# Half-width diagonal score blocks for the linear attention, and idle matmuls in the first half unit of a two-layer trunk

## The chip, the cores and the metric

One core of a Trainium2 chip runs the whole program; the other seven are idle. The metric is the device time of one execution in microseconds (us). TensorE is called PE here, VectorE DVE, ScalarE ACT, GpSimd POOL and SyncE SP, as in the profile; PEld is PE's weight loads.

## What is computed

The reference runs two layers on 256 tokens of width 1024. Each layer projects the normalised input, runs four attention branches of four heads, gates and sums them, and ends with an MLP of squared ReLUs. The change touches the linear-attention branch (GLA), whose scores within a chunk carry a decay for each key channel:

```python
def gla_chunked(q, k, v, log_a):
    ...
    b = jnp.cumsum(_chunk(log_a, c), axis=-2)
    causal = jnp.tril(jnp.ones((c, c), dtype=bool))
    decay = jnp.exp(jnp.where(causal[:, :, None], b[..., :, None, :] - b[..., None, :, :], -jnp.inf))
    scores = jnp.einsum('nbhic,nbhjc,nbhijc->nbhij', qc, kc, decay)
    o_intra = jnp.einsum('nbhij,nbhjd->nbhid', scores, vc)
    ...

def hybrid_layer(...):
    ...
    for n, o in enumerate((o_sb, o_gla, o_dn, o_dil)):
        merged = merged + gates[:, :, n] * (o.reshape(B, S, BRANCH_WIDTH) @ w_branch[n])
    x = x + merged @ w_out
    h = rms_norm(x, g_mlp)
    return x + jnp.square(jax.nn.relu(h @ w_mlp_in)) @ w_mlp_out
```

## The kernel before

Every weight matrix is read once, as a row of "units" (`UNITS`), each of two halves of 512 KB. A half arrives by DMA in a tile `raw` (six buffers). It is then split in two numbers that PE multiplies quickly: ACT casts the upper part `whi` (L254), DVE subtracts it from `raw` for the remainder `wlo` (L255). The activations are split likewise (`ah`, `al`; for a branch's output `oh`, `ol`). PE then makes three products for each half: `whi` by `ah`, `whi` by `al`, `wlo` by `ah`, accumulated in a PSUM bank with the tag `bg`. A gate or projection half is 24 matmuls of 256 columns. `half` asks for splits three halves ahead (`LEAD`).

The attention branches are Python generators (`dn_chain`, `sb_chain`, `dil_chain`, `gla_chain` and helpers) in four threads. `small()` runs after each half unit and advances every thread by one step; `yield from pause(name)` adds as many empty steps as the table `PAUSE` says. The scheduler is off (`manual_schedule`), so this sets the order of each engine's instructions by hand. The order of units in a layer is `SEQ`: projections, then for each branch four gate units and the branch's own unit (`unit_br`), in the order SB, DIL, DN, GLA. `unit_br` first calls `finish(n)`, which forces what is left of that branch's chain, and then multiplies the branch's output by its weights, four pairs of columns (`fp` 0 to 3), each evacuated by DVE (`gt`, L1311).

`gla_chain` builds the transposed scores of a layer in `ST`, a tile of 128 partitions by 3 blocks by 4 heads by 128 columns; blocks 0 and 2 are the diagonal blocks of tokens 0 to 127 and 128 to 255, block 1 the one off the diagonal. POOL clears blocks 0 and 2 (L1070 and the line after it). Coarse blocks are copied from PSUM by ACT. The diagonal and its next neighbours come by two masked copies of DVE (L1110, 128 partitions by 1024 elements each). The levels of 2 to 16 tokens come as small matmuls in the two PSUM banks with the tag `fb`, two heads at a time (`hp` 0 and 1), one bank for each head `b`. For each bank DVE then makes eight masked copies (L1126): four levels, each for the partitions 0 to 63 and 64 to 127, because the two halves write other columns of `ST`. After pause `g9` the second bank follows one step later. The matmuls of `hp` 1 need both `fb` banks again. At the end PE multiplies `v` by `ST` (the only matmuls `fb<-s,sb_k`), and `head_rms` normalises the result: a square on ACT (L584), a sum over heads on PE (`fb<-dlT,C`), `v` on DVE (L593), two activations on ACT (L316, L317), three steps and a product on DVE (L326 to L328, L598), and the split in `oh` (ACT, L474) and `ol` (DVE, L475), which the GLA unit's matmuls read.

At the start of the program, in `trunk`, ten matmuls on a tile of zeros run while the first data are on their way (`WARM`). The first unit (`unit_F` with `boot`) then follows the input and weights as they land, piece by piece, 16 matmuls `whi`/`wlo` by `ah` for its first half (`ft` 0), then 8 by `al`. The masks arrive as f32 in two DMAs of 384 columns and POOL casts them to bytes (L1190).

Of the kernel before, what the change touches and what calls it, by code (L numbers as in the profile page):

```python
# [11 lines left out]
BF = mybir.dt.bfloat16  # L12
U8 = mybir.dt.uint8
# [25 lines left out]
EVU = [3, 3]  # L39
KNOBS = {'SQE': (0, 1), 'CD': (2, 3, 4, 5), 'BSQ': ((2, 2, 2, 2), (2, 0, 2, 0), (0, 0, 0, 0), (2, 2, 0, 0), (0, 2, 0, 0), (2, 0, 0, 0), (1, 2, 2, 0), (1, 2, 0, 0), (2, 2, 0, 1)), 'NPOOL': (0, 1), 'MROWS': (1, 2), 'MADD': ((1, 1, 1, 1), (1, 0, 1, 1), (0, 1, 0, 1), (0, 0, 1, 1), (1, 0, 0, 1)), 'MLO': ((1, 1, 1, 1), (1, 0, 1, 1), (0, 1, 1, 1), (0, 1, 0, 1), (1, 0, 0, 1)), 'DENP': (0, 1), 'TWO': (0, 1), 'ROWS': 'pair', 'TMP': 'pair', 'FLIP': 'pair', 'EVU': 'pair'}  # L40
PAIRS = {'ROWS': (2, 3), 'TMP': (3, 4, 5, 6), 'FLIP': ('dn_v', 'sb_q', 'sb_k'), 'EVU': (0, 1, 2, 3)}
PAUSE = {'m0': 0, 'm1': 0, 'dS': 1, 'd1': 1, 'd2': 2, 'd3': 1, 'd13': 0, 'd14': 0, 'd15': 1, 'd16': 0, 'd17': 2, 'd21': 0, 'd22': 1, 'd23': 1, 'd24': 1, 'd25': 1, 'd26': 0, 'd27': 0, 'd28': 1, 'd29': 0, 'd30': 1, 'd31': 0, 'd32': 1, 'd33': 0, 's0': 2, 's1': 1, 's2': 0, 's3': 1, 's4': 0, 's5': 1, 's6': 0, 's7': 1, 's8': 0, 's9': 1, 's10': 1, 'l0': 2, 'l1': 1, 'l2': 0, 'l3': 1, 'l4': 1, 'l5': 0, 'l6': 2, 'l7': 0, 'l8': 0, 'l9': 2, 'l10': 0, 'l11': 0, 'l12': 1, 'l13': 3, 'g0': 1, 'g1': 0, 'g2': 0, 'g3': 4, 'g4': 1, 'g5': 0, 'g6': 1, 'g7': 1, 'g8': 2, 'g9': 1, 'g10': 0, 'g11': 0, 'fa0': 0, 'fa1': 0, 'fa2': 0, 'fa3': 0, 'fa4': 1, 'fb0': 0, 'fb1': 1, 'fb2': 0, 'fb3': 1, 'fb4': 3, 'd20': 0, 'd34': 0, 'u31': 0, 'u30': 0, 'u29': 0, 'u28': 1, 'u27': 2, 'u26': 0, 'u25': 1, 'u24': 0, 'u23': 0, 'u22': 1, 'u21': 0, 'u20': 2, 'u19': 0, 'u18': 4, 'u17': 2, 'u16': 0, 'u15': 1, 'u14': 0, 'u13': 0, 'u12': 0, 'u11': 1, 'u10': 2, 'u9': 2, 'u8': 0, 'u7': 0, 'u6': 1, 'u5': 0, 'u4': 0, 'u3': 2, 'u2': 0, 'u1': 1, 'dr': 0, 'dl': 1, 'hfa': 1, 'hfb': 0, 'l15': 1, 'e4': 1, 'e5': 0, 'e6': 0, 'e7': 1, 'e8': 0, 'e9': 1, 'e10': 0, 'e12': 0, 'eE0': 2, 'eE1': 0, 'eE2': 1, 'd4': 0, 'e3': 0, 'g12': 1, 'q0': 0, 'q1': 1, 'q2': 1, 'q3': 5, 'q4': 4, 'q5': 0, 'l16': 0, 'l17': 1, 'g13': 0, 'g14': 3, 'g15': 0, 'v_mini': 0, 'v_sb_k': 0, 'v_sb_v': 0, 'v_dil_q': 0, 'v_dil_k': 0, 'v_dil_v': 0, 'v_gla_q': 0, 'v_gla_v': 0, 'v_gla_r': 0, 'v_dn_gate': 0, 'v_dn_v': 0, 'x_hy': 0, 'x_hz': 0, 'x_ht': 0, 'x_x0': 0, 'x_x1': 0, 'x_pt': 0, 'x_s0': 0, 'x_s1': 0, 'x_s2': 0, 'x_ut': 0, 'x_mc': 0}

OFF = {"sb_q": 0, "sb_k": 256, "sb_v": 512, "gla_q": 768, "gla_k": 896, "gla_v": 1024, "gla_lr": 1280,
       "gla_r": 1296, "dn_q": 1552, "dn_k": 1808, "dn_v": 2064, "dn_a": 2320, "dn_b": 2324, "dn_gate": 2328,
# [41 lines left out]
def constants():  # L87
    j = np.arange(128)[:, None]
    i = np.arange(128)[None, :]
    c = np.zeros((128, NCON), np.float32)  # L90
    c[:, C_ID:C_ID + 128] = i == j
    c[:, C_NEGU:C_NEGU + 128] = -1.0 * (j >= i)
    c[:, C_NEG1:C_NEG1 + 128] = -1.0
    c[:, C_UT:C_UT + 128] = j <= i
    c[:, C_GT:C_GT + 128] = j > i
    c[:, C_STR:C_STR + 128] = j < i
    c[:, C_SBN:C_SBN + 128] = np.where(j < i, 0.0, NEG)
    for b, d in enumerate((j - i, j + 128 - i, j - i)):
# [84 lines left out]
def trunk(ctx: ExitStack, tc: tile.TileContext, xin, w, par, con, msk, out, dbg=None, nl=NL):  # L183
# [20 lines left out]
    def mm(o, l, r, start=True, stop=True):  # L204
        PE.matmul(o, l, r, start=start, stop=stop, skip_group_check=True)  # L205
# [354 lines left out]
    def mixing(l, pr, mp, nm):  # L560
# [503 lines left out]
        def gla_chain():  # L1064
# [1 line left out]
            F, qk = got["F"], got["gla_qk"]  # L1066
            yield from pause("g12")
            ST = T([3, 4, 128], "s6")
            POOL.memset(ST[:, 0], 0.0)
            POOL.memset(ST[:, 2], 0.0)  # L1070
            yield from pause("g5")
            for hp in range(2):

                pss = [bank("fb") for _ in range(2)]
                rows = [slice(32 * hh, 32 * hh + 32) for hh in (2 * hp, 2 * hp + 1)]
                for r, ps in zip(rows, pss):
                    mm(ps[:, 0:128], F[r, 0, 0:128], F[r, 0, 128:256])
                for t in range(2):
                    c = 128 * t
                    for r, ps in zip(rows, pss):  # L1080
                        mm(ps[0:64, 128 + 64 * t:192 + 64 * t], F[r, 1, c:c + 64], F[r, 1, c + 64:c + 128])
                for t in range(2):
                    c = 128 * t
                    for b in (0, 64):
                        for r, ps in zip(rows, pss):
                            mm(ps[b:b + 32, 256 + 32 * t:288 + 32 * t], F[r, 2, c + b:c + b + 32],
                               F[r, 2, c + b + 32:c + b + 64])
                yield from pause("g6")
                for hh, ps in zip((2 * hp, 2 * hp + 1), pss):
# [289 lines left out]
```

## Time and profile before

| what | us |
|---|---|
| three runs: median (lowest to highest) | 899.93 (899.72 to 901.83) |
| the profiled execution's own time | 898.36 |
| its span, first to last instruction | 896.5 |
| PE busy in the span | 867.0 (97%) |
| DVE, ACT, POOL busy | 640.8, 537.4, 137.8 |
| mean granted clock of TensorE | 0.98 of 2.4 GHz |

The three parts of the profile used below are the timeline (one line for each run of like instructions: start, length, engine, line, operation, out<-in, number; the bracket is the engine's idle time before it and who ended it), the windows (busy time of each engine in a stretch, and PEclk, the granted clock: 1.00 is 2.4 GHz, 0.50 is 1.2 GHz) and the waits (who waited for whom). Line 205 is the helper of all matmuls, so they are told apart by their operands. An f32 matmul shows as several records.

### The profile page before, as it was taken

The numbers are of one execution on the slowest core, as the hardware profiler recorded it, in microseconds if no ns is written. First come the engines' busy times: TensorE is split into PE (matmuls) and PEld (weight loads), VectorE is DVE, ScalarE is ACT, GpSimd is POOL, SyncE is SP. The second block draws the span as 40 slices with busy tenths as digits, with TensorE's granted clock in tenths as the row PEclk, the third lists the DMA queues.
The fourth block names the chain that finished last, engine by engine and source line by source line (L and its number), as shares of the span: only waits on it lengthen the run. The fifth ranks groups of instructions, "written<-read, shape, count | busy, mean of one in ns | idle before, by whom it ended". The sixth has DMA issues, their size and how long they took to land.

```text
span 896.5 us, 19105 instructions
## 1 busy us (share of the span) xinstructions
PE 867.0 (97%) x7758; PEld 840.4 (94%) x7758; DVE 640.8 (71%) x1272; ACT 537.4 (60%) x846; POOL 137.8 (15%) x142
## 2 busy tenths in 40 slices
PE   7899999998999999999989999999989999999998
PEld 5898999998999999999989899999989999999998
DVE  5878999448788677644488799983596877665442
ACT  4687767855655665633368777696655555664331
POOL 3513401122012000000052341013030120000000
PEclk7899999998999999999999999999999999999999
DMA  8554354543445566665444445554344636667641
GB/s 267 203 157 151 119 189 142 165 142 114 146 145 207 174 202 193 216 219 193 154 158 131 158 135 164 166 159 133 114 140 160 219 122 194 204 204 231 197 148 48
DMA packets 43432, 149.80 MB, mean 167 GB/s; under 512 B 4944, under 2 KB 7248, under 8 KB 43344
## 3 DMA queue, kind: packets, MB, share of 16 engines
q1 hardware_dynamic: 43056, 148.42, 51.1%
q8 instruction: 61, 1.00, 0.5%
q14 instruction: 27, 0.22, 0.1%
q10 hardware_dynamic: 288, 0.17, 0.1%
HBM read 147.52 MB, written 1.05 MB: 166 GB/s over the span
## 4 chain that ended last, share of the span: by engine, by line
PE 72%; DVE 17%; ACT 4%; issue 3%; POOL 2%; DMA 2%; SPq 0%; DVEq 0%; ACTq 0%
PE bg L205 45%; PE fa L205 14%; PE fb L205 12%; DVE wlo L255 5%; DVE al L352 2%; DMA raw<-w 2%; POOL s L382 1%; DVE s L1126 1%; DVE d L706 1%; ACT whi L254 1%; DVE x L516 1%; DVE ush L781 1%; DVE ush L779 1%; DVE Y L783 1%; DVE al L389 1%
## 5 line engine op out<-in xcount | busy, mean ns | idle before, releaser
L255 DVE TENSOR_TENSOR wlo<-raw,whi 128x1024 fp32r<-128x1024 f32 (+2 forms) x280 | 340.9, 1239 | 157.3 <-ACT whi L254 156.8
L254 ACT CAST whi<-raw 128x1024 fp32r<-128x1024 f32 (+2 forms) x280 | 283.4, 1037 | 119.4 <-PE bg L205 60.9
L205 PE MATMUL bg<-ah,whi 128*128 128x256 f32 (+1 forms) x1296 | 316.9, 285 | 3.0 <-ACT whi L254 1.9
L205 PE MATMUL bg<-al,whi 128*128 128x256 f32 (+1 forms) x1296 | 296.6, 279 | 1.8 <-DVE al L352 1.8
L205 PEld LDWEIGHTS bg<-ah,whi 128*128 128x128 f32 (+1 forms) x1296 | 246.0, 190 | 10.5 <-ACT whi L254 3.2
L205 PEld LDWEIGHTS bg<-al,whi 128*128 128x128 f32 (+1 forms) x1296 | 237.9, 189 | 3.2 <-DVE al L352 2.4
L205 PE MATMUL bg<-ah,wlo 128*128 128x256 f32 x1280 | 189.7, 280 | 1.5 <-DVE wlo L255 1.5
L205 PEld LDWEIGHTS bg<-ah,wlo 128*128 128x128 f32 x1280 | 168.5, 191 | 2.6 <-DVE wlo L255 2.5
L205 PE MATMUL fa<-uh,whi 128*128 128x256 f32 x256 | 70.4, 276 | 0.0
L205 PE MATMUL fa<-uh,wlo 128*128 128x256 f32 x256 | 70.4, 276 | 0.0
L205 PE MATMUL fa<-ul,whi 128*128 128x256 f32 x256 | 69.7, 276 | 0.0
L205 PE MATMUL fb<-uh,whi 128*128 128x256 f32 x224 | 61.6, 276 | 0.0
L205 PE MATMUL fb<-uh,wlo 128*128 128x256 f32 x224 | 61.6, 276 | 0.0
L205 PE MATMUL fb<-ul,whi 128*128 128x256 f32 x224 | 61.0, 276 | 0.0
L543 ACT ACTIVATE sq<-rl 128x512 f32<-128x512 f32 x32 | 20.3, 633 | 66.4 <-DVE rl L542 66.4
L1312 POOL TENSOR_TENSOR mg<-mg,gt 128x512 f32<-128x512 f32 x20 | 31.5, 1594 | 150.2 <-DVE gt L1311 150.2
L475 DVE TENSOR_TENSOR ul<-sq,uh 128x512 fp32r<-128x512 f32 x32 | 22.2, 692 | 43.3 <-ACT uh L474 43.3
L205 PEld LDWEIGHTS fa<-uh,wlo 128*128 128x128 f32 x256 | 48.1, 188 | 0.0
L205 PEld LDWEIGHTS fa<-uh,whi 128*128 128x128 f32 x256 | 48.1, 188 | 0.0
L205 PEld LDWEIGHTS fa<-ul,whi 128*128 128x128 f32 x256 | 47.6, 188 | 0.0
L205 PEld LDWEIGHTS fb<-uh,whi 128*128 128x128 f32 x224 | 42.0, 188 | 0.0
L205 PEld LDWEIGHTS fb<-uh,wlo 128*128 128x128 f32 x224 | 42.0, 188 | 0.0
(274 smaller groups left out, 1403.1 us busy)
## 6 DMA issues: line engine op xcount, KB each, us to landing
raw<-w SPq DMA_DIRECT2D x275, 512.0 KB, 4.5
x<-xin SPq DMA_DIRECT2D x3, 256.0 KB, 5.7
out_dram<-x SPq DMA_DIRECT2D x3, 256.0 KB, 2.4
C<-con SPq DMA_DIRECT2D x1, 583.0 KB, 4.4
raw<-w SPq DMA_DIRECT2D x4, 128.0 KB, 5.5
gt<-msk SPq DMA_DIRECT2D x2, 192.0 KB, 5.9
x<-xin SPq DMA_DIRECT2D x2, 128.0 KB, 2.9
raw<-w SPq DMA_DIRECT2D x4, 64.0 KB, 4.2
```

Of the source, the lines that this page charges most:

```text
L205: PE.matmul(o, l, r, start=start, stop=stop, skip_group_check=True)
L254: ACT.copy(hi[:, c], src[:, c])
L255: DVE.tensor_sub(lo[:, c], src[:, c], hi[:, c].bitcast(F32))
L352: DVE.scalar_tensor_tensor(self.h[1][:, kt, :], x[:, kt, :], self.g[:, kt:kt + 1], self.h[0][:, kt, :].bitcast(F32), op0=OP.mult, op1=OP.s ...
L382: POOL.tensor_tensor(t[:, kt, :], x[:, kt, :], self.R, op=OP.mult)
L389: DVE.scalar_tensor_tensor(self.h[1][:, kt, :], self.t[:, kt, :], g, self.h[0][:, kt, :].bitcast(F32), op0=OP.mult, op1=OP.subtract)
L475: DVE.tensor_sub(lo, src, hi.bitcast(F32))
L516: DVE.tensor_add(xs, pairs[fp], xs)
L543: ACT.activation(sq, rl, AF.Square)
L706: DVE.scalar_tensor_tensor(pre[:, b, :], cin[:, b, k:k + 256], cw[:, 4 * b + k:4 * b + k + 1], pre[:, b, :], op0=OP.mult, op1=OP.add)
L779: DVE.stream_shuffle(sh[:, n, k:], uc[:, n, k:], [k] * 32)
L1312: (DVE if n == GLA and MADD[fp] else POOL).tensor_tensor(m, m, g, op=OP.add)
```

## The change

Three parts, with one constant changed.

- **A tile for the diagonal blocks.** `SD`, 128 partitions by 2 blocks by 4 heads by 64 columns, under the tag `sba`, takes for each partition only the 64 columns of its own half. The masks shrink to 64 columns each, so one masked copy does both halves of the partitions, and there are four for each head instead of eight. The two copies of the diagonal write 512 elements instead of 1024. At the end two ACT copies move `SD` into `ST`. POOL clears `SD` and the lower left quarter of `ST`'s diagonal blocks in place of the whole blocks.
- **One step later.** A pause `g11` of one step (the entry was 0 and unused; `PAUSE` differs in nothing else) lies between these ACT copies and the last matmuls of the chain.
- **Idle matmuls.** In the first half unit, `FILL` puts 13 more matmuls on the tile of zeros (128x512 each) between the real ones: 4 ahead of the third `whi`, 3 between it and its `wlo`, 4 ahead of the fifth `whi`, 1 ahead of the seventh and 1 behind it. Their bank is the one of the first ten, which nothing else uses then.
- The masks now come in one DMA of 384 columns, and one POOL cast.

```diff
+FILL = ((0, 0), (0, 0), (4, 3), (0, 0), (4, 0), (0, 0), (1, 1), (0, 0))
...
+    m = np.zeros((128, 6, 64), np.float32)
+    i = 64 * (j // 64) + np.arange(64)[None, :]
...
-    MK = cons.tile([128, 6 * 128], U8, name="MK")
+    MK = cons.tile([128, 6 * 64], U8, name="MK")
...
                 for kt in range(8):
+                    if boot and ft == 0:
+                        state["idle"](FILL[kt][0])
                     mm(ps[:, ft, :], wh[:, kt, :], h[0][:, kt, :], start=kt == 0 and (boot or ft == 0), stop=False)
+                    if boot and ft == 0:
+                        state["idle"](FILL[kt][1])
                     mm(ps[:, ft, :], wl[:, kt, :], h[0][:, kt, :], start=False, stop=False)
...
             ST = T([3, 4, 128], "s6")
-            POOL.memset(ST[:, 0], 0.0)
-            POOL.memset(ST[:, 2], 0.0)
+            SD = T([2, 4, 64], "sba", 2)
+            POOL.memset(SD, 0.0)
+            POOL.memset(ST[64:128, 0:3:2, :, 0:64], 0.0)
...
-                        copy("x_s2", ST[b:b + 32, 0:3:2, hh, b + 32:b + 64], r3(ps[b:b + 32, 256:320], 2))
+                        copy("x_s2", SD[b:b + 32, :, hh, 32:64], r3(ps[b:b + 32, 256:320], 2))
...
-                DVE.copy_predicated(ST[:, 0:3:2], MK3[:, k:k + 1, None, :].to_broadcast([128, 2, 4, 128]), last(dg[:, n], 128))
+                DVE.copy_predicated(SD, MK3[:, k:k + 1, None, :].to_broadcast([128, 2, 4, 64]), last(dg[:, n], 64))
...
                     for o, n in enumerate((3, 4, 5, 6)):
-                        for q in (0, 64):
-                            k = slice(q, q + 64)
-                            DVE.copy_predicated(ST[k, 0:3:2, 2 * hp + b, k], over(MK3[k, 7 - n, k], 2), pss[b][k, o])
+                        DVE.copy_predicated(SD[:, :, 2 * hp + b, :], over(MK3[:, 7 - n, :], 2), pss[b][:, o])
                     yield from pause("g9")
+            for q in (0, 64):
+                k = slice(q, q + 64)
+                ACT.copy(ST[k, 0:3:2, :, k], SD[k])
+            yield from pause("g11")
             yield ("gla_v",)
...
-            for c in range(0, 768, 384):
+            for c in range(0, 384, 384):
...
-        zero = bp.tile([128, 512], BF, name="zero", bufs=1)
+        zero = cons.tile([128, 512], BF, name="zero")
         DVE.memset(zero, 0.0)
         ps = bank("fa")
-        for _ in range(WARM):
-            mm(ps, zero[:, 0:128], zero)
+
+        def idle(n):
+
+            for _ in range(n):
+                mm(ps, zero[:, 0:128], zero)
+
+        idle(WARM)
+        state["idle"] = idle
```

Two places of the order. The first is DVE where the DN branch's unit begins, with the masked copies of `hp` 0; `wlo` is the split of a weight half, `ol` the DN branch's own output, `gt` the evacuation of the first two column pairs. Before:

```order
L475 TENSOR_TENSOR ol<-Y_2674,oh 128x512
L1126 COPY_PREDICATED s_2298<-MK,fb 64x2x64 x8
L255 TENSOR_TENSOR wlo<-raw,whi 128x1024
L1126 COPY_PREDICATED s_2298<-MK,fb 64x2x64 x8
L255 TENSOR_TENSOR wlo<-raw,whi 128x1024
L1311 TENSOR_TENSOR gt<-bg,gt 128x512 x2
```

Changed:

```order
L483 TENSOR_TENSOR ol<-Y_2685,oh 128x512
L1134 COPY_PREDICATED sba<-MK,fb 128x2x64 x4
L259 TENSOR_TENSOR wlo<-raw,whi 128x1024
L1134 COPY_PREDICATED sba<-MK,fb 128x2x64 x4
L259 TENSOR_TENSOR wlo<-raw,whi 128x1024
L1323 TENSOR_TENSOR gt<-bg,gt 128x512 x2
```

The order is the same; each block of copies has half as many. The second place is ACT during GLA's gate units, with the end of GLA's chain: `dlT` is the square of `head_rms`, `s` its two activations, `oh` the split that PE's GLA unit reads, the three `gt` the sigmoid of a gate unit, `whi` the cast of a weight half. Before:

```order
L1284 ACTIVATE gt<-gt 128x512
L584 ACTIVATE dlT_3137<-fb 128x512
L254 CAST whi<-raw 128x1024
L316 ACTIVATE s_3140<-dlT_3139 128x512
L317 ACTIVATE s_3140<-s_3140 128x512
L254 CAST whi<-raw 128x1024
L1282 ACTIVATE gt<-bg 128x512
L1283 ACTIVATE gt<-gt 128x512
L1284 ACTIVATE gt<-gt 128x512
L254 CAST whi<-raw 128x1024
L474 CAST oh<-sbs 128x512
```

Changed:

```order
L1296 ACTIVATE gt<-gt 128x512
L258 CAST whi<-raw 128x1024
L592 ACTIVATE dlT_3164<-fb 128x512
L258 CAST whi<-raw 128x1024
L1294 ACTIVATE gt<-bg 128x512
L1295 ACTIVATE gt<-gt 128x512
L1296 ACTIVATE gt<-gt 128x512
L320 ACTIVATE s_3167<-dlT_3166 128x512
L321 ACTIVATE s_3167<-s_3167 128x512
L258 CAST whi<-raw 128x1024
L482 CAST oh<-sbs 128x512
```

The square and the two activations moved one half unit later, and the two activations now stand behind a gate unit's sigmoid; `oh` stays where it was, ahead of the GLA unit's matmuls.

## Rows read from the trace of the kernel before

**Rows 1.** The profile's part 1: busy us, share of the span, instructions.
```profile
PE 867.0 (97%) x7758; PEld 840.4 (94%) x7758; DVE 640.8 (71%) x1272; ACT 537.4 (60%) x846; POOL 137.8 (15%) x142
```

**Rows 2.** Timeline of PE, layer 0, around the second pair of score matmuls.
```profile
213.64 0.32 PE L205 MATMUL fb<-s 32*64 32x64 f32 x2
216.99 1.98 PE L205 MATMUL fb<-s 32*64 32x64 f32 x62 [3.03 <-DVE s L1126]
...
223.69 0.28 PE L205 MATMUL bg<-ah,whi 128*128 128x256 f32 x1
```

**Rows 3.** Timeline of DVE over the same stretch.
```profile
210.41 2.63 DVE L1126 COPY_PREDICATED s<-MK,fb 64x128 f32<-64x128 uint8 x8
213.07 1.23 DVE L255 TENSOR_TENSOR wlo<-raw,whi 128x1024 fp32r<-128x1024 f32 x1
```

**Rows 4.** Timeline of PE, layer 1, the same place.
```profile
658.18 1.15 PE L205 MATMUL fb<-s 32*64 32x64 f32 x62 [3.02 <-DVE s L1126]
...
663.72 0.28 PE L205 MATMUL bg<-ah,whi 128*128 128x256 f32 x1
```

**Rows 5.** Windows: stretch, busy us (instructions) of five engines, PEclk, DMA share, GB/s.
```profile
8.06:18.30 10.24, 8.42 (x31) 6.92 (x31) 8.55 (x13) 4.90 (x12) 4.61 (x5) 0.50 0.96 325
216.27:223.10 6.83, 6.11 (x81) 5.99 (x82) 5.65 (x8) 0.00 (x0) 3.89 (x3) 0.50 0.46 132
470.00:473.00 3.00, 2.71 (x17) 1.98 (x17) 3.00 (x5) 1.91 (x4) 3.00 (x4) 1.00 0.77 280
503.00:506.00 3.00, 3.00 (x17) 3.00 (x16) 2.47 (x4) 1.60 (x5) 0.00 (x0) 0.50 0.59 157
```

**Rows 6.** Groups of DVE by line and shape: count, busy us, mean ns, idle before.
```profile
L1126 DVE COPY_PREDICATED s<-MK,fb 64x128 f32<-64x128 uint8 x64 | 19.3, 302 | 1.9
...
L1110 DVE COPY_PREDICATED s<-MK,dg 128x1024 f32<-128x1024 uint8 x4 | 5.3, 1334 | 0.1
...
L374 DVE TENSOR_SCALAR nsum<-bg 128x256 f32<-128x256 f32 x4 | 1.7, 423 | 1.4 <-PE bg L205 1.4
...
L1224 DVE SCALAR_TENSOR_TENSOR mini<-bg,nR 64x256 f32<-64x256 f32 x2 | 0.8, 406 | 0.0
```

**Rows 7.** Timeline of PE, layer 1, from the sum over heads to GLA's unit.
```profile
679.12 1.02 PE L205 MATMUL fb<-dlT,C 128*128 128x512 f32 x2
...
685.44 0.28 PE L205 MATMUL bg<-ah,whi 128*128 128x256 f32 x1
...
688.16 0.28 PE L205 MATMUL bg<-oh,whi 128*128 128x256 f32 x1
...
693.20 0.38 PE L205 MATMUL bg<-oh,whi 128*128 128x256 f32 x1 [0.80 <-DVE gt L1311]
```

**Rows 8.** Timeline of DVE, then of ACT, the end of GLA's chain in layer 1.
```profile
680.18 0.69 DVE L593 TENSOR_SCALAR dlT<-fb 128x512 f32<-128x512 f32 x1 [0.72 <-PE fb L205]
...
687.37 0.69 DVE L475 TENSOR_TENSOR ol<-sbs,oh 128x512 fp32r<-128x512 f32 x1
...
680.91 0.64 ACT L316 ACTIVATE s<-dlT 128x512 f32<-128x512 f32 x1 [2.71 <-DVE dlT L593]
...
685.82 0.61 ACT L474 CAST oh<-sbs 128x512 fp32r<-128x512 f32 x1
```

**Rows 9.** Waits of PE from 450 to 560: us in total, times, longest.
```profile
PE fa L205 <- DVE mini L1224: 2.0, 1, 2.0
PE fa L205 <- ACT Y L714: 2.0, 1, 2.0
```

**Rows 10.** Timeline of the start: PE, then DVE, then ACT.
```profile
16.10 0.58 PE L205 MATMUL bg<-ah,wlo 128*128 128x256 f32 x1
...
30.00 0.61 PE L205 MATMUL fa<-C,mini 64*128 64x8 f32 x4 [2.22 <-DVE mini L1224]
...
20.71 0.42 DVE L374 TENSOR_SCALAR nsum<-bg 128x256 f32<-128x256 f32 x1
...
18.48 1.05 ACT L254 CAST whi<-raw 128x1024 fp32r<-128x1024 f32 x1 [4.36 <-DMA raw<-w]
```

More of the change, by code (lines that the diff above doesn't have):

```diff
@@ L41 @@
 PAIRS = {'ROWS': (2, 3), 'TMP': (3, 4, 5, 6), 'FLIP': ('dn_v', 'sb_q', 'sb_k'), 'EVU': (0, 1, 2, 3)}
-PAUSE = {'m0': 0, 'm1': 0, 'dS': 1, 'd1': 1, 'd2': 2, 'd3': 1, 'd13': 0, 'd14': 0, 'd15': 1, 'd16': 0, 'd17': 2, 'd21': 0, 'd22': 1, 'd23': 1, 'd24': 1, 'd25': 1, 'd26': 0, 'd27': 0, 'd28': 1, 'd29': 0, 'd30': 1, 'd31': 0, 'd32': 1, 'd33': 0, 's0': 2, 's1': 1, 's2': 0, 's3': 1, 's4': 0, 's5': 1, 's6': 0, 's7': 1, 's8': 0, 's9': 1, 's10': 1, 'l0': 2, 'l1': 1, 'l2': 0, 'l3': 1, 'l4': 1, 'l5': 0, 'l6': 2, 'l7': 0, 'l8': 0, 'l9': 2, 'l10': 0, 'l11': 0, 'l12': 1, 'l13': 3, 'g0': 1, 'g1': 0, 'g2': 0, 'g3': 4, 'g4': 1, 'g5': 0, 'g6': 1, 'g7': 1, 'g8': 2, 'g9': 1, 'g10': 0, 'g11': 0, 'fa0': 0, 'fa1': 0, 'fa2': 0, 'fa3': 0, 'fa4': 1, 'fb0': 0, 'fb1': 1, 'fb2': 0, 'fb3': 1, 'fb4': 3, 'd20': 0, 'd34': 0, 'u31': 0, 'u30': 0, 'u29': 0, 'u28': 1, 'u27': 2, 'u26': 0, 'u25': 1, 'u24': 0, 'u23': 0, 'u22': 1, 'u21': 0, 'u20': 2, 'u19': 0, 'u18': 4, 'u17': 2, 'u16': 0, 'u15': 1, 'u14': 0, 'u13': 0, 'u12': 0, 'u11': 1, 'u10': 2, 'u9': 2, 'u8': 0, 'u7': 0, 'u6': 1, 'u5': 0, 'u4': 0, 'u3': 2, 'u2': 0, 'u1': 1, 'dr': 0, 'dl': 1, 'hfa': 1, 'hfb': 0, 'l15': 1, 'e4': 1, 'e5': 0, 'e6': 0, 'e7': 1, 'e8': 0, 'e9': 1, 'e10': 0, 'e12': 0, 'eE0': 2, 'eE1': 0, 'eE2': 1, 'd4': 0, 'e3': 0, 'g12': 1, 'q0': 0, 'q1': 1, 'q2': 1, 'q3': 5, 'q4': 4, 'q5': 0, 'l16': 0, 'l17': 1, 'g13': 0, 'g14': 3, 'g15': 0, 'v_mini': 0, 'v_sb_k': 0, 'v_sb_v': 0, 'v_dil_q': 0, 'v_dil_k': 0, 'v_dil_v': 0, 'v_gla_q': 0, 'v_gla_v': 0, 'v_gla_r': 0, 'v_dn_gate': 0, 'v_dn_v': 0, 'x_hy': 0, 'x_hz': 0, 'x_ht': 0, 'x_x0': 0, 'x_x1': 0, 'x_pt': 0, 'x_s0': 0, 'x_s1': 0, 'x_s2': 0, 'x_ut': 0, 'x_mc': 0}
@@ new lines @@
+PAUSE = {'m0': 0, 'm1': 0, 'dS': 1, 'd1': 1, 'd2': 2, 'd3': 1, 'd13': 0, 'd14': 0, 'd15': 1, 'd16': 0, 'd17': 2, 'd21': 0, 'd22': 1, 'd23': 1, 'd24': 1, 'd25': 1, 'd26': 0, 'd27': 0, 'd28': 1, 'd29': 0, 'd30': 1, 'd31': 0, 'd32': 1, 'd33': 0, 's0': 2, 's1': 1, 's2': 0, 's3': 1, 's4': 0, 's5': 1, 's6': 0, 's7': 1, 's8': 0, 's9': 1, 's10': 1, 'l0': 2, 'l1': 1, 'l2': 0, 'l3': 1, 'l4': 1, 'l5': 0, 'l6': 2, 'l7': 0, 'l8': 0, 'l9': 2, 'l10': 0, 'l11': 0, 'l12': 1, 'l13': 3, 'g0': 1, 'g1': 0, 'g2': 0, 'g3': 4, 'g4': 1, 'g5': 0, 'g6': 1, 'g7': 1, 'g8': 2, 'g9': 1, 'g10': 0, 'g11': 1, 'fa0': 0, 'fa1': 0, 'fa2': 0, 'fa3': 0, 'fa4': 1, 'fb0': 0, 'fb1': 1, 'fb2': 0, 'fb3': 1, 'fb4': 3, 'd20': 0, 'd34': 0, 'u31': 0, 'u30': 0, 'u29': 0, 'u28': 1, 'u27': 2, 'u26': 0, 'u25': 1, 'u24': 0, 'u23': 0, 'u22': 1, 'u21': 0, 'u20': 2, 'u19': 0, 'u18': 4, 'u17': 2, 'u16': 0, 'u15': 1, 'u14': 0, 'u13': 0, 'u12': 0, 'u11': 1, 'u10': 2, 'u9': 2, 'u8': 0, 'u7': 0, 'u6': 1, 'u5': 0, 'u4': 0, 'u3': 2, 'u2': 0, 'u1': 1, 'dr': 0, 'dl': 1, 'hfa': 1, 'hfb': 0, 'l15': 1, 'e4': 1, 'e5': 0, 'e6': 0, 'e7': 1, 'e8': 0, 'e9': 1, 'e10': 0, 'e12': 0, 'eE0': 2, 'eE1': 0, 'eE2': 1, 'd4': 0, 'e3': 0, 'g12': 1, 'q0': 0, 'q1': 1, 'q2': 1, 'q3': 5, 'q4': 4, 'q5': 0, 'l16': 0, 'l17': 1, 'g13': 0, 'g14': 3, 'g15': 0, 'v_mini': 0, 'v_sb_k': 0, 'v_sb_v': 0, 'v_dil_q': 0, 'v_dil_k': 0, 'v_dil_v': 0, 'v_gla_q': 0, 'v_gla_v': 0, 'v_gla_r': 0, 'v_dn_gate': 0, 'v_dn_v': 0, 'x_hy': 0, 'x_hz': 0, 'x_ht': 0, 'x_x0': 0, 'x_x1': 0, 'x_pt': 0, 'x_s0': 0, 'x_s1': 0, 'x_s2': 0, 'x_ut': 0, 'x_mc': 0}
@@ L115, in constants @@
         c[r:r + 8, C_AB:C_AB + 8] = np.eye(8)
-    m = np.zeros((128, 6, 128), np.float32)
+    m = np.zeros((128, 6, 64), np.float32)
+    i = 64 * (j // 64) + np.arange(64)[None, :]
     m[:, 5] = i == j
@@ L121, in constants @@
         m[:, n] = up
-    return c, m.reshape(128, 6 * 128)
+    return c, m.reshape(128, 6 * 64)
 def lay_out(inp):
```

## The prediction

> **What bounds the kernel now.** I read part 1 first, then the timeline of PE for its idle times, then the engines that end them, and last the windows for the clock. PE is busy 97% of the span [rows 1], so time is won only where PE stands still or runs at 1.2 GHz. Two places belong to this change. In the DN unit of each layer PE starts the second pair of score matmuls, issues one, and then stands for 3.03 us in layer 0 and 3.02 us in layer 1 until DVE's masked copies have emptied the second `fb` bank [rows 2, 4]. Behind that stall the clock falls: from 216.27 to 223.10 it is at 1.2 GHz [rows 5], and the small matmuls that take 1.15 us in layer 1, where the clock still held for them, take 1.98 us in layer 0 [rows 2, 4]. The other place is the start: from 8.06 to 18.30 PE runs at 1.2 GHz, after gaps in which it waits for the first data [rows 5].
>
> **The masked copies.** Before, a block of eight takes 2.63 us, then a `wlo` 1.23 us, then the second block [rows 3]. A copy of 64 partitions by 128 elements takes 302 ns [rows 6]. After, it is 128 partitions by 128 elements, which the trace does not show as this operation. The lower bound is 302 ns, the upper twice that. I take 302: an operation on 64 partitions by 256 elements takes 406 ns and another on 128 by 256 takes 423 [rows 6], so the partitions cost next to nothing, and the copies of 1024 elements take 1334 ns [rows 6], so it is the elements along a partition that do. Four copies then take 1.32 us (half of 2.63). The first block ends at 211.73, the `wlo` at 213.0, the second block at 214.3. PE's first matmul ends at 213.96 (213.64 and 0.32), so PE waits some 0.38 us instead of 3.03. That is 2.65 us a layer, **5.3 us** for both. The two diagonal copies, at 512 elements, fall from 1334 to about 745 ns (1.15 ns for each element less), 1.2 us of DVE a layer that lies ahead of the same chain. ACT's cast of the next half then holds the chain, so I count nothing for it.
>
> **The clock behind that stall.** From the 62 small records to the next gate unit it takes 6.70 us in layer 0 (216.99 to 223.69) and 5.54 in layer 1 (658.18 to 663.72) [rows 2, 4]. At 2.4 GHz it would be 1.15 for the small matmuls and 2.72 for the 24 matmuls of two column pairs, which is what 24 matmuls of that size take from 685.44 to 688.16 [rows 7]: 3.87. The excess is 2.83 and 1.67, **4.5 us** for both, and it goes if 0.4 us of waiting leaves the clock up. A wait of 0.80 us later in the layer sits in a run of matmuls at full pace [rows 7], so I expect that it does. The ends are 0 and 4.5.
>
> **The end of GLA's chain comes later.** The last matmuls of the chain, the square and the sum over heads move behind one more half unit. The sum goes from 679.12 to about 681.84 [rows 7], and the two activations now stand behind a gate unit's sigmoid, three activations at 0.64 us [rows 8], so the first starts at about 683.8 instead of 680.91. Two activations (1.3 us) and four DVE steps (0.69 each) lead to 688.0. Then DVE has a `wlo` of 1.23 us in its queue and makes `ol` in 0.69 [rows 3, 8]: 689.9. Before, `ol` was ready at 688.06, just before PE's unit began at 688.16 [rows 7, 8]. Now PE waits for it some 1.7 us, with `oh` and `ol` alone late and all of PE's queue behind. A stall of 0.80 us further on in that unit [rows 7] hangs on a cast and a split that were triggered by the half unit before, not by this unit's start, so it is swallowed. Net loss 0.9 us a layer, **1.8 us** for both. The ends are 0 (the chain finds room) and 2.72 a layer (a whole half unit).
>
> **The clock behind the new stall.** The trace has two stalls of 2.0 us in layer 1 [rows 9]. After the one that ended just before 470 the clock stayed at 2.4 GHz, after the other it was at 1.2 GHz at 503 to 506 [rows 5]. A stall of 1.7 us lies just under both, so I count one fall in the two layers. Its price is what the fall in layer 1 cost, **1.7 us**. The ends are 0 and 3.4.
>
> **The idle matmuls.** From 16.10 PE has its data and works at 1.2 GHz until 18.30 [rows 5, 10]. At 2.4 GHz those 2.2 us of work take 1.1, so PE could be 1.1 us earlier. It then comes to a wait of 2.22 us that ends at 30.00, when DVE has made `mini` [rows 10]. That chain does not start at PE: a weight half lands at 18.48, ACT casts it, DVE splits it and only then takes the norm's sum at 20.71, from which its queue runs on to `mini` [rows 10]. PE 1.1 us earlier waits 1.1 us longer. I count **0**, with ends of 1.1 gained and 1.1 lost, the latter if the idle matmuls stand in the way of the real ones and the sum comes late.
> The Trainium skill (TensorE: Matmul & The Clock Gate, Part 1, "What's actually happening") says that throttling is the default state and that activity releases it. By that rule alone the idle matmuls would bring the 1.1 us; by the rows they bring a longer wait.
>
> **The rest.** Two ACT copies of 512 elements cost 1.2 us a layer (0.61 each, as a cast of that size [rows 8]); ACT is busy 60% [rows 1] and its casts run up to three halves ahead of PE, which hides them; uncovered they would cost 2.4 in all. POOL, busy 15% [rows 1], clears less, long before it is needed, and casts one mask instead of two. One mask DMA less frees the queue behind the load that lands at 18.48, where no wait of the page is on a load. I count nothing for these, neither gain nor loss.
>
> **Sum.** 5.3 and 4.5 gained, 1.8 and 1.7 lost: 6.3 us. Against the profiled execution's 898.36 us that is 892.1. The median of the runs is 1.57 us above it, so I predict **893.6** for the median, between 891.9 and 895.3 with no fall of the clock at GLA's unit or one in each layer.
>
> **The rivals.**
> - *The later chain costs nothing.* If ACT or DVE gets to the last steps earlier than I set out, both losses of 3.5 go: 890.1. For it: DVE has 5 us less to do in each layer. Against it: `ol` had only 0.1 us to spare.
> - *The early clock is worth its 1.1 us.* The wait for `mini` would have to shrink too, which needs the DVE queue from 20.71 on to start earlier: 892.5. Against it stands the load at 18.48. This is the outcome of the skill's rule on activity.
> - *The clock falls in the DN unit anyway.* 0.4 us of waiting next to small matmuls of 32 by 64, which may count for little; then only the 5.3 us remain against 3.5 lost: 898.1. For it: in layer 0 the clock stayed down while those small matmuls ran.
> - *The wide copies take twice as long*, so the change does not do what it says. At 604 ns a copy PE waits as before, the excess of 4.5 stays, and the later chain still costs 3.5: 903.4. It decides from about 0.41 us a copy: eight copies ahead of PE then leave 1.2 us of wait, no more than 1.8 is won a layer, and the later chain takes as much. Against it: the pair of 406 and 423 ns.
>
> **How the numbers follow.** A difference under 0.3% (2.7 us) is what a measurement of this kernel can hardly tell from none. Forecast (891.9 to 895.3) 0.60, chain for nothing 0.12, early clock 0.08, clock down anyway 0.15, wide copies 0.05. Faster by over 0.3% (under 897.2) are the first three: 0.80. Within 0.3% is the fourth: 0.15. Slower is the last: 0.05. The range leaves that last case out and reaches from the second case, with most of the early clock's gain on top, to the fourth: 889.3 to 898.4.
>
> **What would show it.** The stall of PE at the second pair of score matmuls under 0.6 us in both layers, four masked copies in 1.3 us, and PEclk 1.00 behind them. A new stall of PE in GLA's unit on `oh` or `ol` of 1 to 2.5 us. At the start PEclk 1.00 to 18 us and a wait for `mini` of over 3 us that still ends at about 30.0. I am wrong if the copies take longer than 0.4 us, if the clock falls behind them all the same, if no stall shows at GLA's unit, or if `mini` is ready clearly before or after 29.9.

## The result and the profile after

| | kernel before | changed kernel |
|---|---|---|
| median beside each other, us (4 runs each) | 899.83 (898.46 to 901.83) | 890.7 (889.01 to 891.34) |
| profiled execution, its span, us | 898.36, 896.5 | 889.01, 887.2 |
| PE busy, mean granted clock | 97%, 0.980 | 98%, 0.988 |

The ratio is 0.9902 (95% interval 0.9887 to 0.9917): 9.1 us faster, where 6.3 were forecast (893.6). Direction and range were right; the gain was larger than the likeliest case.

The copies first. Groups of DVE by line and shape, changed kernel: count, busy us, mean ns, idle before.

```profile
L1134 DVE COPY_PREDICATED sba<-MK,fb 128x128 f32<-128x128 uint8 x32 | 9.7, 303 | 0.8
...
L1120 DVE COPY_PREDICATED sba<-MK,dg 128x512 f32<-128x512 uint8 x4 | 3.0, 740 | 0.1
```

Twice the partitions cost 1 ns against the 302 of [rows 6]; half the elements took the diagonal copies from 1334 to 740 ns. Next the place where PE stood. Timelines of the changed kernel, DVE from layer 0's first block of copies on, then PE in both layers, from the last matmul ahead of the scores to the first one behind the GLA unit (`mh`). The score matmuls stand there as narrow windows cut them:

```profile
211.40 1.32 DVE L1134 COPY_PREDICATED sba<-MK,fb 128x128 f32<-128x128 uint8 x4
212.62 1.22 DVE L259 TENSOR_TENSOR wlo<-raw,whi 128x1024 fp32r<-128x1024 f32 x1
213.76 1.31 DVE L1134 COPY_PREDICATED sba<-MK,fb 128x128 f32<-128x128 uint8 x4
```

```profile
214.33 0.28 PE L209 MATMUL bg<-ol,whi 128*128 128x256 f32 x1
214.76 0.32 PE L209 MATMUL fb<-s 32*64 32x64 f32 x2
215.12 0.39 PE L209 MATMUL fb<-s 32*64 32x64 f32 x10
...
219.05 0.28 PE L209 MATMUL bg<-ah,whi 128*128 128x256 f32 x1
...
244.23 0.38 PE L209 MATMUL bg<-oh,whi 128*128 128x256 f32 x1 [0.57 <-ACT oh L482]
245.31 0.39 PE L209 MATMUL bg<-ol,whi 128*128 128x256 f32 x1 [0.70 <-DVE ol L483]
...
250.77 0.28 PE L209 MATMUL fa<-mh,whi 128*128 128x256 f32 x1
...
648.52 0.28 PE L209 MATMUL bg<-ol,whi 128*128 128x256 f32 x1
...
653.32 0.28 PE L209 MATMUL bg<-ah,whi 128*128 128x256 f32 x1
...
679.03 0.38 PE L209 MATMUL bg<-oh,whi 128*128 128x256 f32 x1 [0.56 <-ACT oh L482]
680.12 0.39 PE L209 MATMUL bg<-ol,whi 128*128 128x256 f32 x1 [0.71 <-DVE ol L483]
...
685.57 0.28 PE L209 MATMUL fa<-mh,whi 128*128 128x256 f32 x1
```

The stall of [rows 2, 4] has shrunk until the profile counts no idle time: PE starts two records at 214.76 and goes on at 215.12, just behind the end of the second block of copies (213.76 and 1.31, 215.07). A new stall stands on `oh` and `ol` in both layers, and the one on `gt` [rows 7] is gone. Windows of the changed kernel (columns as in [rows 5]):

```profile
214.60:220.00 5.40, 5.37 (x100) 5.03 (x99) 5.37 (x8) 3.29 (x4) 3.04 (x2) 1.00 0.59 196
242.00:247.00 5.00, 3.72 (x30) 3.33 (x29) 3.22 (x6) 3.32 (x5) 0.00 (x0) 1.00 0.23 59
648.00:654.00 6.00, 5.97 (x104) 5.63 (x103) 5.90 (x10) 3.81 (x5) 2.86 (x2) 1.00 0.56 186
```

PEclk holds at 1.00 at the scores of both layers and through the new stall (in layer 1 too, from 678 to 685). To add this up, two stretches of PE are measured in each layer: **S** from the last `ol` matmul ahead of the score matmuls to the next gate unit, and **T** from there to that `mh`. For the kernel before the ends that are not in its rows are these (timeline of PE; the gate units begin at 223.69 and 663.72, [rows 2, 4]):

```profile
213.21 0.28 PE L205 MATMUL bg<-ol,whi 128*128 128x256 f32 x1
...
254.69 0.28 PE L205 MATMUL fa<-mh,whi 128*128 128x256 f32 x1
...
654.40 0.28 PE L205 MATMUL bg<-ol,whi 128*128 128x256 f32 x1
...
694.68 0.28 PE L205 MATMUL fa<-mh,whi 128*128 128x256 f32 x1
```

| us | S, layer 0 | S, layer 1 | T, layer 0 | T, layer 1 |
|---|---|---|---|---|
| before | 10.48 | 9.32 | 31.00 | 30.96 |
| changed | 4.72 | 4.80 | 31.72 | 32.25 |
| difference | -5.76 | -4.52 | +0.72 | +1.29 |

S gives 10.28 and T takes 2.01, so 8.27 of the 9.3 us between the two spans lie here. The rest, 1.03, is elsewhere: PE reaches layer 0's S 1.12 later, gains 1.96 between the layers and 0.19 behind T. Windows of the changed kernel and then of the one before show two of these places:

```profile
91.50:94.90 3.40, 3.40 (x18) 3.40 (x17) 3.37 (x6) 2.46 (x5) 2.68 (x4) 0.50 0.07 10
```

```profile
91.50:94.90 3.40, 3.40 (x30) 3.40 (x30) 3.37 (x6) 2.26 (x5) 2.49 (x4) 1.00 0.06 12
615.63:619.04 3.41, 3.41 (x19) 3.29 (x17) 0.05 (x1) 3.21 (x11) 1.90 (x2) 0.50 0.42 150
```

The changed kernel's clock fell at 91.5, the other's did not; the other's fell at 615.6. No edit touches either place, and the same changed kernel executed once more (r1 below) has a PEclk of 1.00 from 91.5 to 94.9 and of 0.59 from 176.8 to 180.2. So these falls differ between executions of one program and are not put down to the change.

### The profile page after: what moved, and what is told of

Same layout as the page of the kernel before. It is cut to its first block, busy times and chain, and to the rows that moved or that the text cites. A ratio compares the mean times of both kernels' runs of the same rounds, so it can differ in the third digit from the quotient of the medians.

```text
span 887.2 us, 19102 instructions
## 1 busy us (share of the span) xinstructions
PE 865.7 (98%) x7771; PEld 837.8 (94%) x7771; DVE 630.0 (71%) x1240; ACT 540.1 (61%) x850; POOL 137.9 (16%) x141
## 4 chain that ended last, share of the span: by engine, by line
PE 73%; DVE 14%; ACT 6%; issue 3%; POOL 2%; DMA 2%; SPq 0%; DVEq 0%; ACTq 0%; POOLq 0%
PE bg L209 46%; PE fa L209 14%; PE fb L209 13%; DVE wlo L259 4%; DVE d L714 2%; DVE al L356 2%; DMA raw<-w 2%; ACT whi L258 1%; POOL s L386 1%; DVE x L524 1%; DVE al L393 1%; POOL sbs L898 1%; ACT Y L397 0%; DVE ush L789 0%; DVE Y L791 0%
```

## The experiments

The account above is theory A: the wide copies alone carry the gain, about half as waiting and half as clock, the idle matmuls are worth nothing and the later step costs a little. The rivals give part of the gain to another part of the change. "Before" and "changed" in a heading tell which kernel an experiment edits. Beside the runs of the three groups (e1 to e4, e5 to e8, r1 to r4) the kernel before had medians of 899.73, 899.61 and 899.34. The ratio need not be that of the two medians: for e5 these give 0.9990.

| run | median us (runs) | ratio to before, 95% interval |
|---|---|---|
| e1_no_fill | 890.29 (6) | 0.9905 [0.9878, 0.9932] |
| e2_no_later_step | 890.19 (6) | 0.9903 [0.9878, 0.9929] |
| e3_fill_alone | 900.02 (12) | 1.0000 [0.9990, 1.0011] |
| e4_later_step_alone | 899.47 (12) | 0.9994 [0.9984, 1.0004] |
| e5_half_copies | 898.74 (12) | 0.9979 [0.9958, 1.0000] |
| e6_copies_together | 886.91 (5) | 0.9864 [0.9841, 0.9888] |
| e7_load_first | 887.93 (6) | 0.9871 [0.9848, 0.9894] |
| e8_load_first_no_fill | 888.86 (5) | 0.9879 [0.9860, 0.9899] |
| r1_change_again | 890.87 (6) | 0.9891 [0.9866, 0.9915] |
| r2_together_again | 891.27 (5) | 0.9891 [0.9869, 0.9913] |
| r3_together_load_first | 888.93 (4) | 0.9865 [0.9838, 0.9892] |
| r4_idle_at_stall | 895.20 (12) | 0.9961 [0.9936, 0.9986] |

### The copies: e5 (changed)

```diff
                     for o, n in enumerate((3, 4, 5, 6)):
-                        DVE.copy_predicated(SD[:, :, 2 * hp + b, :], over(MK3[:, 7 - n, :], 2), pss[b][:, o])
+                        for q in (0, 64):
+                            k = slice(q, q + 64)
+                            DVE.copy_predicated(SD[k, :, 2 * hp + b, :], over(MK3[k, 7 - n, :], 2), pss[b][k, o])
```

> The changed kernel with the masked copies of each level made in two halves of 64 partitions again, eight for each head, into the same tile SD; the rest as changed. Theory A (the number of copies is what mattered): each block takes 2.6 us, the stall of PE at the second pair of score matmuls is back with 2.7 to 3.0 us in both layers, the clock falls behind it, and most of the gain is gone: 898 to 901. Rival (the tile or the shorter diagonal copies brought it): within 2 us of the changed kernel, under 893.

898.74: by the medians 0.9 of the change's 9 us is left, by the ratio 1.9 (interval 0 to 3.8), with every other part in place. DVE's timeline, PE's and the windows of this kernel:

```profile
209.84 2.62 DVE L1136 COPY_PREDICATED sba<-MK,fb 64x128 f32<-64x128 uint8 x8
```

```profile
216.39 1.98 PE L209 MATMUL fb<-s 32*64 32x64 f32 x62 [2.87 <-DVE sba L1136]
...
656.33 1.98 PE L209 MATMUL fb<-s 32*64 32x64 f32 x62 [2.90 <-DVE sba L1136]
```

```profile
217.00:221.00 4.00, 4.00 (x62) 3.88 (x58) 3.73 (x4) 0.00 (x0) 2.60 (x2) 0.50 0.44 135
657.00:661.00 4.00, 4.00 (x63) 3.88 (x56) 3.66 (x4) 0.00 (x0) 2.67 (x2) 0.50 0.39 131
```

The block is 2.62 us again, the stall is back in both layers, and 1.2 GHz stands behind both. S is 10.17 and 10.37. So the number of copies ahead of PE is the cause of the gain in S. The rest of the change together (the tile, the shorter diagonal copies, the two ACT copies, the masks, POOL's clears, the later step, the idle matmuls) is not told from nothing here: between 0 and 3.8 us by the ratio, with the later step's cost (T below) in it.

### The clock behind the stall: r4 (before)

13 matmuls on zeros fill the stall, into a bank that nobody reads. No wait is taken away.

```diff
                 pss = [r4(bank("fb"), 4, 2) for _ in range(2)]
+                if hp:
+                    spare = bank("fa")
+                    for _ in range(13):
+                        mm(spare, state["zero"][:, 0:128], state["zero"])
```

> The kernel before with 13 matmuls on the tile of zeros ahead of the second pair of score matmuls, in the stall of 3 us, and nothing else; the copies and the wait stay. Theory A (half of the gain is the clock behind the stall, not the stall): PE works through the wait, PEclk stays 1.00 behind it, the stretch from the small matmuls to the next gate unit takes 3.9 us in both layers, and the time falls by 3 to 4.5 us: 895.3 to 896.8. Rival (the clock falls for another reason, such as the small matmuls): PEclk 0.50 behind it as before, no gain.

895.20, by the medians 4.1 us faster than before, by the ratio 3.5 (interval 1.3 to 5.8 us). PE's timeline and the windows of this kernel:

```profile
215.51 2.98 PE L205 MATMUL fa<-zero 128*128 128x512 bf16 x13
...
218.95 1.15 PE L205 MATMUL fb<-s 32*64 32x64 f32 x62 [0.21 <-DVE s L1130]
...
656.05 1.15 PE L205 MATMUL fb<-s 32*64 32x64 f32 x62 [0.20 <-DVE s L1130]
...
659.98 0.28 PE L205 MATMUL bg<-ah,whi 128*128 128x256 f32 x1
```

```profile
216.00:220.00 4.00, 3.79 (x76) 2.13 (x74) 3.72 (x10) 1.75 (x2) 0.00 (x0) 1.00 0.40 131
657.00:661.00 4.00, 4.00 (x48) 3.93 (x39) 3.97 (x6) 1.05 (x1) 2.94 (x2) 1.00 0.39 131
```

The data come no earlier, yet the 62 records take 1.15 us in both layers, and the next gate unit starts 3.93 us behind them (656.05 to 659.98) where 3.87 was worked out. S is 7.72 and 7.71. The 62 records start 3.78 us behind the last `ol` matmul in both layers of both kernels (before: 213.21 to 216.99 and 654.40 to 658.18; r4: 215.17 to 218.95 and 652.27 to 656.05), so the wait is the same and only the pace behind it differs. That splits S in its two halves: from before to r4 2.76 and 1.61, together **4.37 of clock** (4.5 forecast); from r4 to the change 3.00 and 2.91, together **5.91 of waiting** (5.3 forecast). The clock's half depends on the execution: with the same stalls of 3.0 us, S is 9.29 and 10.44 in e3 and 9.32 and 9.31 in e4, which would make it 4.30 and 3.20.

### The idle matmuls at the start: e1 (changed), e3 (before)

e1 takes them out; e3 puts only them, with the same numbers, in the kernel before.

```diff
-FILL = ((0, 0), (0, 0), (4, 3), (0, 0), (4, 0), (0, 0), (1, 1), (0, 0))
+FILL = ((0, 0),) * 8
```

> The changed kernel without the 13 idle matmuls. Theory A (all of the gain lies in GLA's copies; the early clock is eaten by the wait for mini): within 0.5 us of the changed kernel, about 890.7, ratio to before 0.990; PE at 1.2 GHz again until about 18.3, the wait for mini about 2.2 us and its end within 0.2 us of 29.9. Theory B (the idle matmuls bring part of it): 1.1 us or more slower than the changed kernel, 891.8 or above.

> The kernel before with the 13 idle matmuls and nothing else. Theory A: 899.8, ratio 1.000 within 0.0007, the clock up early and the wait for mini longer by about as much as PE comes earlier. Theory B: 898.7 or less, ratio 0.9988 or less.

e1's median is 0.4 us below the change's, e3's 0.3 above before. For e3 the interval leaves at most 0.9 us of gain; e1's is wider, some 2.4 us to either side. e3's window and PE's timeline show that the clock did what it was asked to, and that nobody gained by it; the two lines behind are the changed kernel's own clock and its wait for `mini`:

```profile
8.00:18.00 10.00, 8.13 (x50) 5.78 (x49) 8.20 (x13) 5.28 (x13) 4.26 (x5) 1.00 0.98 335
```

```profile
18.27 0.59 PE L207 MATMUL bg<-nsum,C 128*128 128x256 f32 x2
...
29.03 0.73 PE L207 MATMUL fa<-C,mini 64*128 64x8 f32 x4 [2.55 <-DVE mini L1230]
```

```profile
13.00:16.40 3.40, 3.40 (x15) 3.08 (x15) 3.40 (x6) 0.73 (x3) 1.75 (x3) 0.50 0.90 276
```

```profile
29.86 0.86 PE L209 MATMUL fa<-C,mini 64*128 64x8 f32 x4 [2.62 <-DVE mini L1236]
```

In e3 the clock is at 2.4 GHz through the whole stretch. By the rule of the Trainium skill that activity releases the throttle (TensorE: Matmul & The Clock Gate, Part 1, "What's actually happening") that is as it should be, and the trace of e3 agrees; the time does not follow. In the changed kernel's profile the same idle matmuls did not hold the clock throughout: it is at 1.2 GHz from 13.0 to 16.4. Why the time does not follow, six executions show together. `load` is the start of ACT's cast of the awaited weight half, `sum` the start of PE's `nsum` matmuls, `mini` the end of PE's wait:

| kernel | load | sum | mini | mini - load |
|---|---|---|---|---|
| before [rows 10] | 18.48 | 19.86 | 30.00 | 11.52 |
| changed | 18.35 | 18.76 | 29.86 | 11.51 |
| e1 | 18.59 | 20.11 | 30.11 | 11.52 |
| e3 | 17.51 | 18.27 | 29.03 | 11.52 |
| r1 (the change once more) | 18.37 | 18.25 | 29.88 | 11.51 |
| e5 | 17.40 | 19.37 | 29.31 | 11.91 |

In the first five PE's sum moves by 1.86 us between the earliest and the latest, and `mini` stays 11.5 us behind the load. In e5 the load came early and PE's sum late; there DVE waits 0.28 us for PE, and `mini` comes 9.94 us behind PE's sum. So the later of the two sets it. In the kernel before they were close: 9.94 behind its sum is 29.80, and `mini` came at 30.00.

### The load moved: e7 (changed), e8 (e7 without `FILL`)

`CD` is the number of weight halves whose loads SP issues ahead of the constants; the awaited one becomes the last of them.

```diff
-CD = 3
+CD = 4
```

> The changed kernel with one weight half more loaded ahead of the constants (CD 4), so that the half that landed at 18.5 us lands some 1.5 us earlier. Theory A (that load, not PE, sets when mini is ready): the cast of that half starts 1 to 2 us earlier, PE's wait for mini ends 0.8 to 1.5 us earlier, and the time falls by as much, 889.2 to 889.9. Rival (PE or POOL sets it): the wait ends within 0.3 us of 29.8, no difference.

> The same without the idle matmuls. Theory A: with the load earlier the sum of the norm waits for PE, which is then 1.1 us later without the idle matmuls, so here the idle matmuls are worth 0.5 to 1.1 us: 890.2 to 890.9. Rival (the start is not bound by the load): the same as with them within 0.3 us.

e7's timeline, ACT, DVE and PE:

```profile
13.32 1.05 ACT L258 CAST whi<-raw 128x1024 fp32r<-128x1024 f32 x1 [0.37 <-DMA raw<-w]
```

```profile
18.83 0.42 DVE L378 TENSOR_SCALAR nsum<-bg 128x256 f32<-128x256 f32 x1 [1.36 <-PE bg L209]
```

```profile
18.20 0.59 PE L209 MATMUL bg<-nsum,C 128*128 128x256 f32 x2
...
28.13 0.61 PE L209 MATMUL fa<-C,mini 64*128 64x8 f32 x4 [1.98 <-DVE mini L1236]
```

The load came 5.0 us earlier (18.35 to 13.32) where 1.5 were expected. DVE now waits for PE, and `mini` follows PE's sum: 9.93 us behind it here, 9.94 in e8 (18.78 to 28.72) and in r3 (18.81 to 28.75). PE's wait ends 1.73 us earlier than in the change, and both medians lie 1.3 us below what was expected. Whether the idle matmuls count now is not shown: e7 with them is 0.6 us ahead of e8 in `mini`, but r3, which has them too, is level with e8, and the intervals of e7 and e8 overlap. The load alone seems worth some 2 us: three kernels with it (e7, e8, r3) have 887.9 to 888.9, the change 890.7 and 890.9. The intervals overlap here too, and e6, without the early load, had 886.9, so this is indicated, not settled.

### The later step: e2 (changed, without it), e4 (before, with it)

```diff
-'g11': 1
+'g11': 0
```

e4 sets `yield from pause("g11")`, at 1, ahead of `gla_v` in the kernel before.

> The changed kernel with g11 back at 0, so that the last matmuls of GLA's chain stand one half unit earlier, behind the ACT copies. Theory A (the later step costs a stall of 1.3 us on oh and ol and saves one of 0.8): the stall on oh and ol goes, the one of 0.8 us on gt comes back, 0.5 us a layer, 889.7. Rival (the ACT copies are then late for the last matmuls): a new stall of PE at fb<-s,sb_k of 1 us or more, and 891 or above.

> The kernel before with one pause of a step ahead of the last matmuls of GLA's chain and nothing else. Theory A: a stall on oh and ol of 1 to 2 us at each GLA unit in place of the 0.8 us on gt, 0.5 to 1 us a layer, 901 to 902, ratio about 1.001 to 1.002. Rival (DVE, which is busier here, makes it much later): over 2.5 us a layer, 905 or above.

The waits moved as expected; the waits of PE in e4 from 225 to 300 (us in total, times, longest):

```profile
PE bg L205 <- DVE ol L475: 0.7, 1, 0.7
PE bg L205 <- ACT oh L474: 0.6, 1, 0.6
```

In e2 it is the other way round, the 0.8 on `gt` is back. T is 31.71 in both layers of e4 and 31.00 and 30.96 in e2: the step costs 0.71 to 0.75 us a layer in either kernel. The time does not show it. For e2 its 1.45 us lie inside the interval. For e4 they do not: it should be 1.45 slower and is 0.3 faster, with an interval that ends at 0.4 slower. That expectation missed. In e4's profiled execution layer 0 lost less to the clock behind its old stall (S 9.32 against 10.48). That happens without this edit too: e3, which changes only the start, has 9.29 there. Whether it accounts for the median stays open.

### The copies of `hp` 1 in one step: e6, r1, r2, r3

e6 and r2 drop the pause between the two blocks of copies of `hp` 1 in the changed kernel, so the chain ends a step earlier. r1 is the changed kernel, r3 is e6 with `CD = 4`.

```diff
-                    yield from pause("g9")
+                    if not (hp and b == 0):
+                        yield from pause("g9")
```

> The changed kernel with the masked copies of the second pair of heads in one step instead of two, so that the rest of GLA's chain, the later step included, moves one half unit forward. Theory A: as with g11 at 0, the stall on oh and ol goes and the one of 0.8 us on gt comes back: 889.7, 0.5 us a layer. Rival (2.6 us of copies in one piece hold up a split of a weight half): a stall of PE on wlo of 1 us or more and no gain.

> The changed kernel itself, beside the next two on the same chip. Every theory: 890 to 891.5, ratio 0.990 within 0.001; it is the yardstick for the next two.

> The kernel with the second pair's masked copies in one step again. Theory A (it saves 0.5 us a layer at GLA's unit, and the rest of what was seen was where the clock happened to fall): 0.5 to 1.5 us faster than the changed kernel here. Rival (the order saves more, about 3.8 us as in the first runs): 3 us or more faster.

> Both: the second pair's masked copies in one step and one weight half more loaded ahead of the constants. If the two gains are of separate places they add up: faster than the one with the copies together by the 1 to 2.5 us that the earlier load brought, 884.5 to 886.5. If the earlier load's gain was only a luckier place of the clock's falls: no difference.

In e6 the stall on `oh` and `ol` is gone and the 0.8 on `gt` is back, and it seemed 3.8 us better than the change. The same kernel again, r2, is not (891.27 against 890.87): the gain was not reproduced, and I take no version as shown to beat the change. r2 had been expected 0.5 to 1.5 us below r1 and r3 at 884.5 to 886.5; both came out slower than that. The windows of e6 and then of r2 show what differed:

```profile
91.50:94.90 3.40, 3.40 (x29) 3.40 (x30) 3.37 (x6) 2.19 (x5) 2.42 (x4) 1.00 0.01 2
176.80:180.20 3.40, 3.40 (x32) 3.21 (x32) 0.33 (x1) 2.92 (x11) 1.69 (x2) 1.00 0.44 117
```

```profile
91.50:94.90 3.40, 3.40 (x18) 3.40 (x17) 3.37 (x6) 2.56 (x6) 2.82 (x4) 0.50 0.09 13
176.80:180.20 3.40, 3.40 (x21) 3.28 (x19) 0.00 (x0) 3.15 (x11) 2.05 (x2) 0.50 0.44 146
```

One program, two executions, and falls of the clock that one has and the other has not (a third is at 613.7 to 617.1). Differences of 1 to 2 us between kernels can't be told apart here by the median of a few runs; a stretch of the timeline can.

## Why the prediction was right, and where not

| step of the prediction | forecast us | measured us | shown by |
|---|---|---|---|
| waits at the second pair of scores | -5.3 | -5.91 | S of r4 and of the change |
| clock behind them | -4.5 | -4.37 | S of before and of r4 |
| later end of GLA's chain, net | +1.8 | +1.44 | T of layer 0, twice; T of e4, e2 |
| one fall of the clock behind that stall | +1.7 | 0 | windows |
| idle matmuls | 0 | 0 | e1, e3 |
| masks, POOL, ACT copies | 0 | none seen (0 to 3.8 with the other parts) | e5 |
| falls and pace elsewhere | none | -0.46 | left over: spans (-1.03), and +0.57 in T of layer 1 |
| sum | -6.3 | -9.3 | |

- **The copies** were right in price (302 taken, 303 measured) and so in everything behind it. The waits are worth a little more than forecast: from the start of the first two records to that of the third it was 3.35 us (213.64 to 216.99) and is now 0.36, 2.99 less where 2.65 were taken. Of the 0.38 us of waiting that the sum left, nearly all is gone. The two blocks and the `wlo` between them ran in 3.67 us (211.40 to 215.07) where 3.89 were added up (210.41 to 214.3), and PE came to the scores 3.36 us behind the start of the first block, before 3.23.
- **The clock at the scores** was right, and r4 shows the term by itself. The rival in which the clock falls in the DN unit anyway is refuted, and that of copies twice as long by their 303 ns.
- **The later chain** was right in mechanism and nearly in size. The prediction had PE waiting some 1.7 us. The two idle times add to 1.27, but the starts are 1.70 late in layer 1: eight `wlo` matmuls from 677.40 would let the unit start at 678.31 (0.91, as from 687.25 to 688.16 before), it starts at 679.03, and `ol` follows 1.09 behind `oh` in place of 0.11. The old stall on `gt`, 0.80 of idle time, had made starts 0.96 late. The rival in which the chain costs nothing is refuted in its mechanism, since the profile shows the stalls; its time, 890.1, is near the result because of the next point.
- **The step that failed** is "I count one fall in the two layers". The stall was likened to the two of 2.0 us in [rows 9], of which one was followed by a fall. It comes as 0.57 and 0.70 with an `oh` matmul between, and no fall followed: PEclk is 1.00 behind this stall in both layers of all seven profiles that have it (the change, e1, e4, e5, e7, e8, r1). Whether its shortness or the matmul in its middle kept the clock up stays open. That is 1.7 of the 3.0 us by which the profiled execution beat its forecast. The waits give 0.6 more and the cheaper chain 0.4, the clock at the scores 0.1 less, and some 0.5 is left for the clock and the pace elsewhere, which no step had counted.
- **Luck.** Without that fall the prediction's own sum is 891.9. The median lies 1.2 us below this, and single executions of the changed kernel lie further apart than that (887.16 to 893.98 in r1). The stated range reached down to 889.3 only because of the two rivals of 890.1 and 892.5, and both are refuted.
- **The idle matmuls** came out as said in what they are worth: PE's sum came 1.1 us earlier (19.86 to 18.76), the wait for `mini` ended at 29.86 (30.0 forecast) because here the load sets it. The wait did not grow to over 3 us, only to 2.62, and PEclk did not hold to 18 us: in the changed kernel's profile it is at 1.2 GHz from 13.0 to 16.4. The rival of the early clock is refuted as long as the load is the later of the two.

## What to carry to other kernels

Count a masked copy of DVE by the elements along a partition (here 302 ns for 64 partitions, 303 for 128): two copies that differ only in their partitions are one copy, if a tile can be laid out so that both write the same columns. A stall of PE can be paid twice, as waiting and in the clock behind it: the stalls of 3.0 us here cost 1.6 to 2.8 us of clock each, those of 0.57 and 0.70 none. Idle matmuls that filled the long ones won the second half back without touching their cause. Speed ahead of a wait is worth something only on the chain that ends the wait: measure the distance from each candidate over several kernels. The one whose distance stays constant (here 11.5 us from the load) is the one to move, until another becomes the later (here PE's sum, 9.94 us ahead).

## What was not expected of the hardware

**Matmuls run at two paces at a granted clock of 1.00.** In e1's profiled execution (897.8, the longest of its six) the last part is 4% slower than in the change, with the same PEclk and PE busy throughout. Windows of the change and then of e1:

```profile
740.00:880.00 140.00, 140.00 (x1238) 140.00 (x1237) 77.51 (x77) 65.31 (x75) 0.00 (x0) 1.00 0.54 174
```

```profile
740.00:880.00 140.00, 140.00 (x1191) 140.00 (x1191) 78.40 (x77) 67.53 (x77) 0.00 (x0) 1.00 0.55 178
```

140 us hold 1238 matmuls there (113.1 ns each) and 1191 here (117.5). No records are merely missing: half units start 2.72 us apart there and 2.83 here. The same pace explains the 0.57 us in T of layer 1 of the change, and it is not the change's doing, for r1, the same kernel, has the 31.72 of layer 0 there. The timeline of PE in the change:

```profile
655.21 1.10 PE L209 MATMUL bg<-ah,wlo 128*128 128x256 f32 x8
658.03 1.10 PE L209 MATMUL bg<-ah,wlo 128*128 128x256 f32 x8
...
674.68 1.07 PE L209 MATMUL bg<-ah,wlo 128*128 128x256 f32 x8
677.40 1.07 PE L209 MATMUL bg<-ah,wlo 128*128 128x256 f32 x8
```

A half unit takes 2.82 us and then 2.72. What sets the pace stays open; it was not tried.

**Matmuls on zeros can hold the clock up**: the windows of e3 and r4 above show PEclk 1.00 over stretches that are at 0.50 without them. They did not always: in the profile of the change, which has those of e3, PEclk was 0.50 from 13.0 to 16.4.
